# Low key parts on both halves: every score product of three attentions over 128 partitions

## The chip, the cores and the metric

The kernel runs on one core of one Trainium2 chip, in one launch. The metric is device time in microseconds (us) of that launch; lower is better. Three runs of the kernel before gave 981.36 us as their median (980.42 to 981.79). The engines are called PE (TensorE), DVE (VectorE), ACT (ScalarE), POOL (GpSimd) and SP (SyncE); PEld is PE's loading of a product's first operand, which overlaps with the products.

## The reference

Two transformer blocks over 256 tokens of 1024 numbers, in f32. The first has an attention with three branches (compressed, selected, windowed; 8 query heads, 2 key groups of 64), a recurrent branch and an MLP; the second has a neighbourhood attention (8 heads of 64), an attention over a band with a sink (8 query heads, 2 key heads), and two gated MLPs. The lines that matter here are the scores:

```python
qc = lax.dynamic_slice_in_dim(qh, t0, Q_CHUNK, axis=3)
s = jnp.einsum('bgrcd,bgcnd->bgrcn', qc, ksel) * ATTN_SCALE          # selected, first block
s = jnp.einsum('bgrcd,bgnd->bgrcn', qc, kw) * ATTN_SCALE             # windowed, first block
s = jnp.einsum('bchd,bicjhd->bhcij', q_r, k_g).astype(jnp.float32) * scale + bias   # second block, a
s = jnp.einsum('bnqhgd,bnkhd->bnhgqk', qb, kb).astype(jnp.float32) * (dh ** -0.5)   # second block, b
```

A head has 64 numbers, so each score is a sum over 64.

## The kernel before, in words

Features lie on partitions, tokens on the free axis. PE multiplies the type F32R, so each f32 operand is split in a high part (`ACT` copies it into F32R) and a low part (`DVE` subtracts the copy from the original). The weights stream in by SP's queue as pieces of 1024 columns, and `split_to` makes `whi` (ACT, L248) and `wlo` (DVE, L249) of each piece; five buffers of each hold the pieces that are split ahead. A product of features and weights is three products: high by high, low by high, high by low (L300, L294; in the MLPs L306 and L307).

**Scores.** A query tile `q(s, i)` has head s's high part on its own 64 partitions (`HALF[s]`) and its low part on the other 64, so that one product over 128 partitions with the key's high part `kh(s)`, which `put_k` writes on both halves (L585, L586, ACT), gives high by high plus low by high. The key's low part `kl` lies on head s's own half alone (L587, DVE), and the third product, high by low, runs over those 64 partitions: `q(s, i)[HALF[s]]` by `kl[HALF[s]]`. Each call of `scores2` (L767, neighbourhood attention `na_scores` and band attention `gq_scores`, four of each) makes 4 products over 128 partitions (L773) and 4 over 64 (L775); `nsa_scores` (L813) does the same for the first block, L824 and L826, with 4 and 4 (u=0, j of 4) or 2 and 2 (u=1). So there are 56 products over 128 partitions and 56 over 64, all with 256 columns. The scores of s=0 and s=1 go into the two buffers of the PSUM pool "s", which the masks (L784, DVE) read.

**Where the parts lie.** In the first block the key tile `k_1` also holds `pch` and `pcl` (the compressed attention's probabilities); `vc_parts` (tag "side") holds compressed values. In the second block `kal` lies behind the values in `va`'s two tiles, and `kb_vb` (tag "side") holds `kbh`, `kbl` and the band's values. `mix_fin` (L1247) writes the cosines and sines times the norm into a tile `cossin` of its own, which `rope_tile` reads. The pool "big" has 12 buffers of 128x2048 words.

**Order of the work.** `ORDER_1` and `ORDER_2` (L156, L159) list the steps, attention steps ("at") between projections; a scheduler that has its own model of time then sets the order on each engine.

Of the kernel before, what the change touches and what calls it, by code (L numbers as in the profile page):

```python
# [8 lines left out]
F32 = mybir.dt.float32  # L9
F32R = mybir.dt.float32r  # L10
AF = mybir.ActivationFunctionType
ALU = mybir.AluOpType
AX = mybir.AxisListType

P = 128
T = 256
# [358 lines left out]
def build(nc, tc, d, out, es, dbg=None):  # L375
# [22 lines left out]
    G = Prog(nc, tc, pools, d, dbg)  # L398
    one = pools["one"]
    V = {}  # L400
    S = {}
# [111 lines left out]
    def v2(b):  # L513
        return b.rearrange("p (k t) -> p k t", k=2)
# [67 lines left out]
    def put_k(kh, kl, t):  # L582
        for s in range(2):
            own, other = HALF[s], HALF[1 - s]
            nc.scalar.activation(out=kh(s)[own], in_=t[own], func=AF.Copy)  # L585
            nc.scalar.activation(out=kh(s)[other], in_=t[own], func=AF.Copy)  # L586
            nc.vector.tensor_tensor(out=kl[own], in0=t[own], in1=kh(s)[own].bitcast(F32), op=ALU.subtract)  # L587

    def ev_q(p, b):
        if p == 0:  # L590
# [5 lines left out]
    def ev_k(p, b):  # L596
        t = G.big("k_1", F32R, (P, 2048))
        S["kh"] = t[:, 0:1024].rearrange("p (s b t) -> p s b t", s=2, b=2)
        S["kl"] = t[:, 1024:1536].rearrange("p (b t) -> p b t", b=2)
        S["pch"], S["pcl"] = t[:, 1536:1792], t[:, 1792:2048]  # L600
        t = G.tmp("k_sb")
        nc.vector.tensor_tensor(out=v2(t), in0=v2(b), in1=two(S["rbA"]), op=ALU.mult)
        put_k(lambda s: S["kh"][:, s], S["kl"], v2(t))

    W1 = "w_in"

# [99 lines left out]
    def cmp_w2():  # L706
        hid = S["cmp_hid"]
        rep = G.tmp("cmp_rep")[:, :256].rearrange("p (h r c) -> p h r c", h=2, r=4)
        nc.vector.tensor_copy(rep, hid[:, 1, :, None, :].to_broadcast([P, 2, 4, 32]))
        b = G.ps("t", "cmpo")  # L710
        for ht in range(2):
            nc.tensor.matmul(b[:, 0:32], V["w2k"][:, ht, :], hid[:, 0, ht, :], start=ht == 0, stop=ht == 1)
        for ht in range(2):
            nc.tensor.matmul(b[:, 64:128], rep[:, ht].rearrange("p r c -> p (r c)"), V["w2v"][:, ht, :],
                             start=ht == 0, stop=ht == 1, skip_group_check=True)
        kc = b[:, 0:32].rearrange("p (s n) -> p s n", s=2)
        kl = G.small((P, 32), "kcl").rearrange("p (s n) -> p s n", s=2)
        G.split2(S["kc"][:, :, 0:16], kl, kc, 0.5)
        nc.vector.tensor_tensor(out=S["kc"][:, :, 16:32], in0=kl, in1=S["kcmask"].rearrange("p (s n) -> p s n", s=2), op=ALU.mult)
        vc = G.tmp("vc")  # L720
        nc.vector.tensor_tensor(out=vc.rearrange("p (s c) -> p s c", s=8), in0=b[:, None, 64:128].to_broadcast([P, 8, 64]),
                                in1=S["vcmask"][:, :, None].to_broadcast([P, 8, 64]), op=ALU.mult)
        t = one.tile([P, 1536], F32R, tag="side", name="vc_parts")
        S["vch"], S["vcl"] = t[:, 0:512], t[:, 512:1024]
        G.split2(S["vch"], S["vcl"], vc, 0.5)

    def gate_cols(j=None):
# [39 lines left out]
    def scores2(name, q, kh, kl):  # L767

        bs = [G.ps("s", f"S{name}{s}") for s in range(2)]
        for i in range(2):  # L770
            o = slice(i * T, i * T + T)
            for s in range(2):
                nc.tensor.matmul(bs[s][:, o], q(s, i), kh(s), start=True, stop=False, skip_group_check=True)  # L773
            for s in range(2):
                nc.tensor.matmul(bs[s][:, o], q(s, i)[HALF[s]], kl[HALF[s]], start=False, stop=True, skip_group_check=True)  # L775
        return bs

    def softmax(name, segs, post):
# [34 lines left out]
    def nsa_scores(u, j):  # L813
        nm_ = f"n{u}{j}"
        kh, kl, n = S["kh"], S["kl"], 3 if u == 0 else 1
        qs = lambda s, i: S["q"][:, s, j, i * P:(i + 1) * P]
        bs = [G.ps("s", f"S{nm_}{s}") for s in range(2)]
        if u == 0:
            parts = [(lambda s: bs[s][:, 0:T], 0, lambda k: k[:, :, 0:P]), (lambda s: bs[s][:, T:2 * T], 1, lambda k: k[:, 0, :])]
        else:  # L820
            parts = [(lambda s: bs[s][:, 0:T], 1, lambda k: k[:, 1, :])]
        for o, i, keys in parts:
            for s in range(2):
                nc.tensor.matmul(o(s), qs(s, i), keys(kh[:, s]), start=True, stop=False, skip_group_check=True)  # L824
            for s in range(2):
                nc.tensor.matmul(o(s), qs(s, i)[HALF[s]], keys(kl)[HALF[s]], start=False, stop=True, skip_group_check=True)  # L826
        first, second = S["causal"][:, 0:P], S["causal"][:, P:3 * P]
        if u == 0:
            t = pools["att"].tile([P, 2, 512], F32, tag="att", name="att" + nm_)
            segs = [(t[:, s, o:o + w], bs[s][:, o:o + w], m, False) for s in range(2)  # L830
                    for o, w, m in ((0, P, first), (P, P, first), (T, T, second))]
            g = S["gA"][:, j]
        else:
            t = pools["half"].tile([P, 2, T], F32, tag="half", name="att" + nm_)
            segs = [(t[:, s], bs[s][:, 0:T], second, False) for s in range(2)]
            g = S["gB"][:, j]

        def fin(sm):
            f = G.small((P, 2 * n), "f" + nm_)
            nc.vector.tensor_scalar(out=sm, in0=sm, scalar1=1e-20, scalar2=None, op0=ALU.max)  # L840
            nc.vector.reciprocal(f, sm)
            nc.vector.tensor_tensor(out=f, in0=f, in1=g, op=ALU.mult)
            return f

        softmax(nm_, segs, lambda nm: fin)
        S[f"at{u}{j}"] = t
# [399 lines left out]

    def mix_fin():  # L1247
        norm_fin("acc1", "A")
        cs = one.tile([P, 2, T], F32, tag="cossin", name="cossin")
        S["cossin"] = cs  # L1250
        nc.vector.tensor_tensor(out=cs[:, 0, :], in0=S["cos"], in1=S["rbA"], op=ALU.mult)
        nc.vector.tensor_tensor(out=cs[:, 1, :], in0=S["sin"], in1=S["rbA"], op=ALU.mult)

    def ev_qa(p, b):
        if p == 0:
# [5 lines left out]
    def ev_ka(p, b):  # L1261
        if p == 0:
            S["kah"] = G.big("ka", F32R, (P, 2, 4, T))
            va_ = [G.big("va" + n, F32R, (P, 2048)) for n in ("hi", "lo")]
            S["vah"], S["val"] = (v[:, 0:1536].rearrange("p (i j c) -> p i j c", i=2, j=4) for v in va_)
            S["kal"] = [v[:, 1536:2048].rearrange("p (j t) -> p j t", j=2) for v in va_]
        t = G.tmp(f"ka{p}")
        nc.vector.tensor_tensor(out=v2(t), in0=v2(b), in1=two(S["rbA"]), op=ALU.mult)
        put_k(lambda s: S["kah"][:, s, 2 * p:2 * p + 2, :], S["kal"][p], v2(t))

    def rope_tile(name, b, scale):

        t = G.tmp("rt" + name)[:, :T]
        nc.scalar.activation(out=t, in_=b, func=AF.Copy, scale=scale)
        rb = G.ps("t", "rot" + name)
        nc.tensor.matmul(rb[:, :T], S["rot"], t, start=True, stop=True)
        u = G.tmp("ru" + name)[:, :T]
        nc.vector.tensor_tensor(out=u, in0=rb[:, :T], in1=S["cossin"][:, 1, :], op=ALU.mult)
        nc.vector.tensor_tensor(out=t, in0=t, in1=S["cossin"][:, 0, :], op=ALU.mult)
        nc.vector.tensor_tensor(out=t, in0=t, in1=u, op=ALU.add)  # L1280
        return t

# [26 lines left out]

    def va():  # L1310

        sd = one.tile([P, 1536], F32R, tag="side", name="kb_vb")
        S["vbh"], S["vbl"] = (sd[:, 768 + 384 * a:1152 + 384 * a].rearrange("p (i c) -> p i c", i=2) for a in range(2))
        S["kbh"], S["kbl"] = sd[:, 0:2 * T].rearrange("p (s t) -> p s t", s=2), sd[:, 2 * T:3 * T]
        for t in (S["vah"], S["val"]):
            nc.gpsimd.memset(t[:, :, :, 64:128].bitcast(F32), 0.0)
        for t in (S["vbh"], S["vbl"]):
# [18 lines left out]
    def kb():  # L1336
        bk = G.ps("g", "kb")
        for k in range(8):
            wh, wl = G.wt(("kb", k))
            G.mmx(bk[:, :T], wh, wl, x3(k), k == 0, k == 7)  # L1340
        put_k(lambda s: S["kbh"][:, s, :], S["kbl"], rope_tile("k", bk[:, :T], 1.0))

    def full_softmax(name, bs, mask, post):
        t = pools["att"].tile([P, 2, 512], F32, tag="att", name="att" + name)
# [3 lines left out]

    def na_scores(j):
        nm_ = f"a{j}"  # L1350
        bs = scores2(nm_, lambda s, i: S["qa"][:, s, j, i * P:(i + 1) * P], lambda s: S["kah"][:, s, j, :], S["kal"][j // 2][:, j % 2, :])

        def mask(s, i):
            e = 2 if i == 0 else 0
# [10 lines left out]

    def gq_scores(j):
        nm_ = f"b{j}"
        bs = scores2(nm_, lambda s, i: S["qb"][:, s, j, i * P:(i + 1) * P], lambda s: S["kbh"][:, s, :], S["kbl"])
        sk = S["sink"].rearrange("p (s j) -> p s j", s=2)[:, :, j:j + 1].to_broadcast([P, 2, 2])

        def post(nm):
# [213 lines left out]
```

## Time and profile before

| | |
|---|---|
| median of three runs | 981.36 us |
| the profiled execution | 979.5 us |
| its span, first to last instruction | 977.7 us |
| mean granted TensorE clock | 0.996 |
| PE busy | 962.3 us (98%) |
| DVE busy | 729.8 us (75%) |
| ACT busy | 580.4 us (59%) |

The profiled execution lies 1.9 us under the median of the three runs, and 1.8 us of it lie outside the span. Busy time of PE counts overlapping products once; a product's own length is longer than the step to the next product's start, so costs on PE are read from starts. Times within the execution are us from the span's start: the first block's attention lies between 44 and 200, the second block's between 626 and 740.

### The profile page before, as it was taken

The page shows a single profiled execution, that of the slowest core. Times are in us where ns is not written, and L with a number is a line of the kernel's source. Part 1 is how long each engine was busy: PE and PEld are TensorE (multiplying, and loading weights), DVE is VectorE, ACT ScalarE, POOL GpSimd, SP SyncE. Part 2 cuts the span into 40 slices and gives each one's busy share as a digit, 9 for nine tenths or more (in the row PEclk, how much of TensorE's full clock was granted, in tenths as well). Part 3 has the DMA queues.
Part 4 walks back from the last instruction along what each step waited for, and adds up shares of the span by engine and source line. Part 5 has one row for each costly group of instructions (what it writes and reads, how often), then busy time and mean ns, then how long its engine had stood idle before and what let it go on. Part 6 is the DMA issues. An engine that isn't in the chain of part 4 may idle for free.

```text
span 977.7 us, 15978 instructions
## 1 busy us (share of the span) xinstructions
PE 962.3 (98%) x6310; PEld 874.2 (89%) x6310; DVE 729.8 (75%) x1219; ACT 580.4 (59%) x953; POOL 40.1 (4%) x71
## 2 busy tenths in 40 slices
PE   8999999999999999999999999899999999999997
PEld 7999999998888888888888889899899888888897
DVE  7898779778888655679888667678767878777553
ACT  6784897446766544556555444667664566555541
POOL 6100000000000000030000200000000000000000
PEclk9999999999999999999999999999999999999999
DMA  9584333634555545565555655353225565554541
GB/s 330 182 294 180 133 127 130 226 144 174 195 193 180 208 173 200 188 205 193 195 178 208 207 189 192 128 173 120 85 99 174 196 211 175 199 186 172 180 152 44
DMA packets 26555, 174.03 MB, mean 178 GB/s; under 512 B 3312, under 2 KB 3568, under 8 KB 7280
## 3 DMA queue, kind: packets, MB, share of 16 engines
q1 hardware_dynamic: 24912, 169.80, 49.0%
q0 software_dynamic: 1136, 2.63, 1.4%
q8 instruction: 49, 0.80, 0.3%
q10 hardware_dynamic: 432, 0.58, 0.2%
q14 instruction: 26, 0.21, 0.1%
HBM read 171.43 MB, written 1.05 MB: 176 GB/s over the span
## 4 chain that ended last, share of the span: by engine, by line
PE 97%; DVE 1%; DMA 1%; ACT 0%; issue 0%; SPq 0%; POOL 0%; POOLq 0%
PE f L306 17%; PE w L306 12%; PE f L307 8%; PE w L307 6%; PE ld L294 6%; PE ga L300 5%; PE gb L300 5%; PE fd L306 4%; PE wo L306 3%; PE gr L300 2%; PE m1b L300 2%; PE xr L300 2%; PE fd L307 2%; PE wo L307 2%; PE va L294 1%; PE ka L300 1%
## 5 line engine op out<-in xcount | busy, mean ns | idle before, releaser
L249 DVE TENSOR_TENSOR wlo<-raw,whi 128x1024 fp32r<-128x1024 f32 (+3 forms) x322 | 388.9, 1210 | 169.9 <-ACT whi L248 152.4
L248 ACT ACTIVATE whi<-raw 128x1024 fp32r<-128x1024 f32 (+3 forms) x322 | 336.0, 1048 | 301.4 <-PE w L306 64.1
L306 PE MATMUL f<-u,whi 128*128 128x512 f32 x704 | 246.7, 396 | 0.0
L307 PE MATMUL f<-u,wlo 128*128 128x256 f32 x704 | 196.9, 280 | 0.0
L306 PEld LDWEIGHTS f<-u,whi 128*128 128x128 f32 x704 | 132.2, 188 | 31.2
L307 PEld LDWEIGHTS f<-u,wlo 128*128 128x128 f32 x704 | 132.9, 189 | 0.1
L306 PE MATMUL w<-u,whi 128*128 128x512 f32 x256 | 88.8, 392 | 0.0
L306 PE MATMUL w<-hid,whi 128*128 128x512 f32 x256 | 88.8, 391 | 0.0
L307 PE MATMUL w<-hid,wlo 128*128 128x256 f32 x256 | 71.9, 281 | 0.0
L307 PE MATMUL w<-u,wlo 128*128 128x256 f32 x256 | 71.5, 281 | 0.0
L306 PE MATMUL fd<-f1h,whi 128*128 128x512 f32 x176 | 61.1, 394 | 0.0
L294 PE MATMUL ld<-whi,f2h 128*128 128x256 f32 (+1 forms) x264 | 59.1, 319 | 0.0
L306 PEld LDWEIGHTS w<-hid,whi 128*128 128x128 f32 x256 | 47.9, 187 | 10.4
L306 PEld LDWEIGHTS w<-u,whi 128*128 128x128 f32 x256 | 47.8, 187 | 10.2
L300 PE MATMUL gb<-u,whi 128*128 128x256 f32 x256 | 50.2, 288 | 0.0
L300 PE MATMUL ga<-u,whi 128*128 128x256 f32 x256 | 49.1, 287 | 0.0
L307 PE MATMUL fd<-f1h,wlo 128*128 128x256 f32 x176 | 48.9, 278 | 0.0
L307 PEld LDWEIGHTS w<-u,wlo 128*128 128x128 f32 x256 | 48.5, 190 | 0.2
L307 PEld LDWEIGHTS w<-hid,wlo 128*128 128x128 f32 x256 | 48.5, 190 | 0.0
L294 PEld LDWEIGHTS ld<-whi,f2h 128*128 128x128 f32 x264 | 44.1, 191 | 3.4
L306 PE MATMUL wo<-m,whi 128*128 128x512 f32 x128 | 44.4, 394 | 0.0
L294 PE MATMUL ld<-wlo,f2h 128*128 128x256 f32 (+1 forms) x132 | 42.1, 320 | 0.0
(534 smaller groups left out, 1919.3 us busy)
## 6 DMA issues: line engine op xcount, KB each, us to landing
raw<-in_ws_dram SPq DMA_DIRECT2D x150, 1024.0 KB, 4.9
raw<-in_ws_dram SPq DMA_DIRECT2D x3, 960.0 KB, 4.8
raw<-in_ws_dram SPq DMA_DIRECT2D x2, 992.0 KB, 4.9
nar<-in_rpb_dram POOLq DMA_DIRECT2D x16, 96.0 KB, 5.9
raw<-in_ws_dram SPq DMA_DIRECT2D x4, 256.0 KB, 6.7
raw<-in_ws_dram SPq DMA_DIRECT2D x2, 512.0 KB, 7.4
raw<-in_ws_dram SPq DMA_DIRECT2D x1, 932.0 KB, 5.3
res<-in_x_dram SPq DMA_DIRECT2D x2, 384.0 KB, 6.5
```

What stands on the lines that cost most here:

```text
L248: self.hi_ins.append(nc.scalar.activation(out=hi[:, :w], in_=src, func=AF.Copy))
L249: nc.vector.tensor_tensor(out=lo[:, :w], in0=src, in1=hi[:, :w].bitcast(F32), op=ALU.subtract)
L294: mm(out, a, b, start=start and r == 0, stop=stop and r == 2, skip_group_check=True)
L300: mm(out, a, b, start=start and r == 0, stop=stop and r == 2, skip_group_check=True)
L306: mm(bank.rearrange("p (a t) -> p a t", a=2), wh, x, start=start, stop=False, skip_group_check=True)
L307: mm(bank[:, :T], wl, x[:, 0, :], start=False, stop=stop, skip_group_check=True)
```

## The change

`put_k` writes the low part too on both halves: DVE's subtraction now comes right after the first high copy, and a new ACT copy (L588 of the changed kernel) carries it to the other half. Both kinds of scores then take all of `q(s, i)` and all of `kl(s)`, so that the second product, too, runs over 128 partitions (it adds low by low), and they go through s outside and i inside. The low parts need twice the room: `kl` of the first block takes the place of `pch` and `pcl`, which move to `vc_parts`; `kal` gets a tile of its own in the pool "big"; the tag "side" grows from 1536 to 1792 words; the cosines and sines are multiplied in place, and `cossin` goes.

```diff
@@ put_k
             nc.scalar.activation(out=kh(s)[own], in_=t[own], func=AF.Copy)
+            nc.vector.tensor_tensor(out=kl(s)[own], in0=t[own], in1=kh(s)[own].bitcast(F32), op=ALU.subtract)
             nc.scalar.activation(out=kh(s)[other], in_=t[own], func=AF.Copy)
-            nc.vector.tensor_tensor(out=kl[own], in0=t[own], in1=kh(s)[own].bitcast(F32), op=ALU.subtract)
+            nc.scalar.activation(out=kl(s)[other], in_=kl(s)[own].bitcast(F32), func=AF.Copy)
@@ ev_k
-        S["kl"] = t[:, 1024:1536].rearrange("p (b t) -> p b t", b=2)
-        S["pch"], S["pcl"] = t[:, 1536:1792], t[:, 1792:2048]
+        S["kl"] = t[:, 1024:2048].rearrange("p (s b t) -> p s b t", s=2, b=2)
@@ cmp_w2
-        t = one.tile([P, 1536], F32R, tag="side", name="vc_parts")
+        t = one.tile([P, 1792], F32R, tag="side", name="vc_parts")
         S["vch"], S["vcl"] = t[:, 0:512], t[:, 512:1024]
+        S["pch"], S["pcl"] = t[:, 1024:1280], t[:, 1280:1536]
@@ scores2
-        for i in range(2):
-            o = slice(i * T, i * T + T)
-            for s in range(2):
+        for s in range(2):
+            for i in range(2):
+                o = slice(i * T, i * T + T)
                 nc.tensor.matmul(bs[s][:, o], q(s, i), kh(s), start=True, stop=False, skip_group_check=True)
-            for s in range(2):
-                nc.tensor.matmul(bs[s][:, o], q(s, i)[HALF[s]], kl[HALF[s]], start=False, stop=True, skip_group_check=True)
+                nc.tensor.matmul(bs[s][:, o], q(s, i), kl(s), start=False, stop=True, skip_group_check=True)
@@ nsa_scores
-        for o, i, keys in parts:
-            for s in range(2):
+        for s in range(2):
+            for o, i, keys in parts:
                 nc.tensor.matmul(o(s), qs(s, i), keys(kh[:, s]), start=True, stop=False, skip_group_check=True)
-            for s in range(2):
-                nc.tensor.matmul(o(s), qs(s, i)[HALF[s]], keys(kl)[HALF[s]], start=False, stop=True, skip_group_check=True)
+                nc.tensor.matmul(o(s), qs(s, i), keys(kl[:, s]), start=False, stop=True, skip_group_check=True)
@@ mix_fin
-        cs = one.tile([P, 2, T], F32, tag="cossin", name="cossin")
...
+        for k in ("cos", "sin"):
+            nc.vector.tensor_tensor(out=S[k], in0=S[k], in1=S["rbA"], op=ALU.mult)
@@ ev_ka
-            S["kal"] = [v[:, 1536:2048].rearrange("p (j t) -> p j t", j=2) for v in va_]
+            S["kal"] = G.big("kal", F32R, (P, 2, 4, T))
@@ va
-        sd = one.tile([P, 1536], F32R, tag="side", name="kb_vb")
...
+        sd = one.tile([P, 1792], F32R, tag="side", name="kb_vb")
...
```

The orders on POOL and SP stay as they were. On PE, DVE and ACT the scheduler moves steps within the two attentions' stretches; two places matter.

PE, the scores of the neighbourhood attention's third pair of heads (`Sa`; `ka` and `valo` or `kal` are the key's high and low parts, `ga` a gate's projection beside it). Before:

```order
L300 MATMUL ga_7015<-u_0_5878,whi_6809 128x256
L773 MATMUL Sa_6988<-ka,qa 128x256
L775 MATMUL Sa_6988<-valo,qa 128x256
L773 MATMUL Sa_6988<-ka,qa 128x256
L775 MATMUL Sa_6988<-valo,qa 128x256
L773 MATMUL Sa_6989<-ka,qa 128x256
L775 MATMUL Sa_6989<-valo,qa 128x256
```

The same place in the changed kernel (its L774 and L775 are the high and the low product):

```order
L300 MATMUL ga_7021<-u_0_5880,whi_6815 128x256 x2
L774 MATMUL Sa_6994<-ka,qa 128x256
L775 MATMUL Sa_6994<-kal,qa 128x256
L774 MATMUL Sa_6994<-ka,qa 128x256
L775 MATMUL Sa_6994<-kal,qa 128x256
L300 MATMUL ga_7021<-u_0_5880,wlo_6816 128x256
L300 MATMUL ga_7021<-u_0_5880,whi_6815 128x256 x2
L300 MATMUL ga_7021<-u_0_5880,wlo_6816 128x256
L774 MATMUL Sa_6995<-ka,qa 128x256
```

High and low products alternate in both; products of the gate now stand between s=0 and s=1, and the number of score products is the same.

ACT, just after the first block's keys: weight parts (`whi`), the new copies, and the exponentials (`attn`) of the first scores. Before:

```order
L248 ACTIVATE whi_641<-raw_470 128x840
L248 ACTIVATE whi_655<-raw_535 128x840
L917 ACTIVATE xc<-xr_593,vec 128x256 x2
L248 ACTIVATE whi_675<-raw_535 128x560
L268 ACT_TABLE_LOAD
...
L268 ACTIVATE attn_1134,smn_1138<-attn_1134,nmn_1135 128x256 x2
L248 ACTIVATE whi_756<-raw_653 128x1024
L248 ACTIVATE whi_804<-raw_653 128x1024
```

The same place in the changed kernel (L588 is the new copy; buffer numbers are 2 higher):

```order
L248 ACTIVATE whi_643<-raw_472 128x840
L588 ACTIVATE k_460<-k_460 64x512 x2
L248 ACTIVATE whi_657<-raw_537 128x840
L248 ACTIVATE whi_677<-raw_537 128x560
...
L268 ACT_TABLE_LOAD
...
L248 ACTIVATE whi_758<-raw_655 128x1024
L268 ACTIVATE attn_1136,smn_1140<-attn_1136,nmn_1137 128x256
L248 ACTIVATE whi_806<-raw_655 128x1024
```

Up to `whi_804` (now `whi_806`) ACT has two copies of 64x512 more and one exponential of 128x256 less; the exponential follows later. On PE the last products of the compression's first layer (`cmph`), which use the weight part after these, now stand 16 rows of the gate's projection later.

## Rows read from the trace of the kernel before

**Rows 1.** The page: busy time of PE with its share; the chain's shares by engine.

```profile
PE 962.3 (98%) x6310; PEld 874.2 (89%) x6310; DVE 729.8 (75%) x1219; ACT 580.4 (59%) x953; POOL 40.1 (4%) x71
...
PE 97%; DVE 1%; DMA 1%; ACT 0%; issue 0%; SPq 0%; POOL 0%; POOLq 0%
```

**Rows 2.** Instructions of lines L826 and L775: count, duration (ns) min/median/max, starts.

```profile
L826 PE MATMUL Sn<-k,q x24: 379/382/382, 44.8 to 174.0; 64*128 64x256 f32 x24
...
L775 PE MATMUL Sb<-kb_vb,qb x16: 379/382/386, 683.8 to 709.0; 64*128 64x256 f32 x16
...
L775 PE MATMUL Sa<-vahi,qa x8: 380/381/383, 626.6 to 653.5; 64*128 64x256 f32 x8
...
L775 PE MATMUL Sa<-valo,qa x8: 379/380/382, 657.7 to 672.0; 64*128 64x256 f32 x8
```

**Rows 3.** Timeline of PE, third pair of `a`: start us, us, engine, line, tiles, count.

```profile
657.50 0.28 PE L773 MATMUL Sa<-ka,qa 128*128 128x256 f32 x1
657.71 0.38 PE L775 MATMUL Sa<-valo,qa 64*128 64x256 f32 x1
658.02 0.39 PE L773 MATMUL Sa<-ka,qa 128*128 128x256 f32 x1
...
659.59 0.38 PE L775 MATMUL Sa<-valo,qa 64*128 64x256 f32 x1
...
660.12 0.28 PE L300 MATMUL ga<-u,wlo 128*128 128x256 f32 x1
660.24 0.40 PE L300 MATMUL ga<-u,whi 128*128 128x256 f32 x2
```

**Rows 4.** Timeline of PE, scores of the first block at 163.

```profile
162.82 0.40 PE L824 MATMUL Sn<-k,q 128*128 128x256 f32 x2
163.15 0.39 PE L826 MATMUL Sn<-k,q 64*128 64x256 f32 x2
163.46 0.51 PE L824 MATMUL Sn<-k,q 128*128 128x256 f32 x2
163.90 0.38 PE L826 MATMUL Sn<-k,q 64*128 64x256 f32 x2
...
164.55 0.28 PE L300 MATMUL gb<-u,wlo 128*128 128x256 f32 x1
```

**Rows 5.** Timeline of PE: first and last of the rows with two 64-partition products.

```profile
45.38 0.38 PE L826 MATMUL Sn<-k,q 64*128 64x256 f32 x2
...
690.55 0.39 PE L775 MATMUL Sb<-kb_vb,qb 64*128 64x256 f32 x2
```

**Rows 6.** Timeline of PE, 50 to 62; in brackets idle time and its releaser.

```profile
50.92 0.40 PE L294 MATMUL vg<-wlo,u 128*128 128x280 f32 x1 [0.32 <-DVE wlo L249]
...
58.93 0.50 PE L300 MATMUL ga<-u,whi 128*128 128x256 f32 x2
...
61.37 0.34 PE L673 MATMUL cmph<-whi,cmpB 128*64 128x256 f32 x1 [1.09 <-ACT whi L248]
```

**Rows 7.** Timeline of ACT: a key copy, an exponential, two weight pieces.

```profile
42.23 0.63 ACT L586 ACTIVATE k<-k_sb 64x512 fp32r<-64x512 f32 x1
...
56.33 0.49 ACT L268 ACTIVATE attn<-attn,nmn 128x256 f32<-128x256 f32 x1
...
56.87 2.01 ACT L248 ACTIVATE whi<-raw 128x1024 fp32r<-128x1024 f32 x2
```

**Rows 8.** Busy time by stretch: length; PE, PEld, DVE, ACT, POOL; clock, DMA.

```profile
50.00:75.00 25.00, 23.59 (x188) 22.73 (x188) 24.97 (x48) 20.70 (x40) 1.50 (x4) 1.00 0.85 307
150.00:175.00 25.00, 25.00 (x196) 23.64 (x195) 24.62 (x52) 21.32 (x40) 0.00 (x0) 1.00 0.44 158
```

**Rows 9.** ACT's longest wait in 62 to 175: total us, times, longest.

```profile
ACT whi L248 <- PE xr L300: 5.2, 3, 3.0
```

**Rows 10.** Timeline of PE behind its longest wait in the second block.

```profile
619.15 0.77 PE L300 MATMUL ka<-u,whi 128*128 128x256 f32 x2 [3.31 <-DVE qa L1258]
```

**Rows 11.** Writers of tile `tga`, 640 to 740: count, duration, first and last start.

```profile
L1411 DVE SCALAR_TENSOR_TENSOR tga<-ga,rb_A x3: 682/692/693, 666.6 to 694.9; 128x512 f32<-128x512 f32 x3
```

More of the change, by code (lines that the diff above doesn't have):

```diff
@@ L598, in ev_k @@
         S["kh"] = t[:, 0:1024].rearrange("p (s b t) -> p s b t", s=2, b=2)
-        S["kl"] = t[:, 1024:1536].rearrange("p (b t) -> p b t", b=2)
-        S["pch"], S["pcl"] = t[:, 1536:1792], t[:, 1792:2048]
+        S["kl"] = t[:, 1024:2048].rearrange("p (s b t) -> p s b t", s=2, b=2)
         t = G.tmp("k_sb")
         nc.vector.tensor_tensor(out=v2(t), in0=v2(b), in1=two(S["rbA"]), op=ALU.mult)
-        put_k(lambda s: S["kh"][:, s], S["kl"], v2(t))
+        put_k(lambda s: S["kh"][:, s], lambda s: S["kl"][:, s], v2(t))
     W1 = "w_in"
@@ L1248, in mix_fin @@
         norm_fin("acc1", "A")
-        cs = one.tile([P, 2, T], F32, tag="cossin", name="cossin")
-        S["cossin"] = cs
-        nc.vector.tensor_tensor(out=cs[:, 0, :], in0=S["cos"], in1=S["rbA"], op=ALU.mult)
-        nc.vector.tensor_tensor(out=cs[:, 1, :], in0=S["sin"], in1=S["rbA"], op=ALU.mult)
+        for k in ("cos", "sin"):
+            nc.vector.tensor_tensor(out=S[k], in0=S[k], in1=S["rbA"], op=ALU.mult)
     def ev_qa(p, b):
@@ L1265, in ev_ka @@
             S["vah"], S["val"] = (v[:, 0:1536].rearrange("p (i j c) -> p i j c", i=2, j=4) for v in va_)
-            S["kal"] = [v[:, 1536:2048].rearrange("p (j t) -> p j t", j=2) for v in va_]
+            S["kal"] = G.big("kal", F32R, (P, 2, 4, T))
         t = G.tmp(f"ka{p}")
         nc.vector.tensor_tensor(out=v2(t), in0=v2(b), in1=two(S["rbA"]), op=ALU.mult)
-        put_k(lambda s: S["kah"][:, s, 2 * p:2 * p + 2, :], S["kal"][p], v2(t))
+        put_k(lambda s: S["kah"][:, s, 2 * p:2 * p + 2, :], lambda s: S["kal"][:, s, 2 * p:2 * p + 2, :], v2(t))
     def rope_tile(name, b, scale):
@@ L1277, in rope_tile @@
         u = G.tmp("ru" + name)[:, :T]
-        nc.vector.tensor_tensor(out=u, in0=rb[:, :T], in1=S["cossin"][:, 1, :], op=ALU.mult)
-        nc.vector.tensor_tensor(out=t, in0=t, in1=S["cossin"][:, 0, :], op=ALU.mult)
+        nc.vector.tensor_tensor(out=u, in0=rb[:, :T], in1=S["sin"], op=ALU.mult)
+        nc.vector.tensor_tensor(out=t, in0=t, in1=S["cos"], op=ALU.mult)
         nc.vector.tensor_tensor(out=t, in0=t, in1=u, op=ALU.add)
@@ L1310, in va @@
     def va():
-        sd = one.tile([P, 1536], F32R, tag="side", name="kb_vb")
-        S["vbh"], S["vbl"] = (sd[:, 768 + 384 * a:1152 + 384 * a].rearrange("p (i c) -> p i c", i=2) for a in range(2))
-        S["kbh"], S["kbl"] = sd[:, 0:2 * T].rearrange("p (s t) -> p s t", s=2), sd[:, 2 * T:3 * T]
+        sd = one.tile([P, 1792], F32R, tag="side", name="kb_vb")
+        S["vbh"], S["vbl"] = (sd[:, 1024 + 384 * a:1408 + 384 * a].rearrange("p (i c) -> p i c", i=2) for a in range(2))
+        S["kbh"], S["kbl"] = (sd[:, 512 * a:512 * a + 512].rearrange("p (s t) -> p s t", s=2) for a in range(2))
         for t in (S["vah"], S["val"]):
@@ L1340, in kb @@
             G.mmx(bk[:, :T], wh, wl, x3(k), k == 0, k == 7)
-        put_k(lambda s: S["kbh"][:, s, :], S["kbl"], rope_tile("k", bk[:, :T], 1.0))
+        put_k(lambda s: S["kbh"][:, s, :], lambda s: S["kbl"][:, s, :], rope_tile("k", bk[:, :T], 1.0))
     def full_softmax(name, bs, mask, post):
@@ L1350, in na_scores @@
         nm_ = f"a{j}"
-        bs = scores2(nm_, lambda s, i: S["qa"][:, s, j, i * P:(i + 1) * P], lambda s: S["kah"][:, s, j, :], S["kal"][j // 2][:, j % 2, :])
+        bs = scores2(nm_, lambda s, i: S["qa"][:, s, j, i * P:(i + 1) * P], lambda s: S["kah"][:, s, j, :], lambda s: S["kal"][:, s, j, :])
         def mask(s, i):
@@ L1367, in gq_scores @@
         nm_ = f"b{j}"
-        bs = scores2(nm_, lambda s, i: S["qb"][:, s, j, i * P:(i + 1) * P], lambda s: S["kbh"][:, s, :], S["kbl"])
+        bs = scores2(nm_, lambda s, i: S["qb"][:, s, j, i * P:(i + 1) * P], lambda s: S["kbh"][:, s, :], lambda s: S["kbl"][:, s, :])
         sk = S["sink"].rearrange("p (s j) -> p s j", s=2)[:, :, j:j + 1].to_broadcast([P, 2, 2])
```

## The prediction

> **What bounds the kernel now.** I read the page first. PE is busy for 98% of the span and the chain of work that ended last runs through PE for 97% of it [rows 1]: whatever shortens the row of products shortens the kernel, as long as the other engines keep ahead. Next, the instructions of the two low product lines: 56 products over 64 partitions, each 0.38 us long [rows 2]. That length says little, since products overlap; the timeline of PE gives the steps from start to start. Two neighbouring products over 128 partitions with 256 columns start 0.12 us apart (660.12 and 660.24 in [rows 3]). Around a low product this is different: the step into it is 0.21 us, the step out of it 0.31 us [rows 3]. Where two low products stand side by side, one on each half, a row with both is as long as one alone, 0.38 or 0.39 us [rows 4, 5], so they run at the same time; but the way in and out is paid there too. Last come the waits and busy times by stretch, which tell where PE has a margin. The list of PE's waits is empty between 62 and 175 and between 625 and 710, while ACT waits for PE there to hand back weight buffers [rows 9]: PE sets the pace. Between 44 and 62 it does not: PE waits 0.32 us for a low weight part and 1.09 us for a high one [rows 6], with DVE busy 24.97 of 25 us in the stretch from 50 [rows 8].
>
> **The sum, part by part.** *A low product that stands alone.* From 657.50 to 660.12 there are 8 score products, four of them lone low ones, and one gate product: 2.62 us [rows 3]. Nine steps of 0.12 make 1.08. The other 1.54 us are four visits to half height, 0.385 us each.
>
> *Two that stand together.* From 162.82 to 164.55 there are 8 score products with two such couples, and two gate products: 1.73 us [rows 4]. Ten steps make 1.20, so a couple costs 0.53 / 2 = 0.265 us more than two full products would.
>
> The Trainium skill's page "TensorEngine Tiling (Array Packing)", Key Properties, says that changing the tiling mode drains TensorE; by that rule the cost sits at the change of height, and the steps of 0.21 and 0.31 us agree.
>
> *How many.* Twelve rows of the timeline hold a couple, the first at 45.38 and the last at 690.55 [rows 5]; the other 32 of the 56 stand alone. They fall in three stretches: 4 alone and 1 couple up to 51 (1.54 + 0.27 = 1.8 us), 12 alone and 3 couples from 96 to 174 (4.62 + 0.80 = 5.4 us), 16 alone and 8 couples from 626 to 709 (6.16 + 2.12 = 8.3 us). The sum is 15.5 us.
>
> In the changed kernel all 56 are full products behind a full product with the same first operand. The trace has none of exactly this kind. The bounds are 0.12 us, the step of any full product into the same bank, and 0.31 us, the step at a low one. I take 0.12: first and second operand then have the shape of the gate's products, whose step that is.
>
> *The last two stretches.* I let 5.4 and 8.3 us count whole: 13.7 us. The cover is that weight parts, probabilities and masks must come 6 or 7% sooner there. ACT's waits for PE of up to 3.0 us [rows 9] are room of that kind; the tightest stretch is 150 to 175, with DVE busy 24.62 of 25 us [rows 8]. New waits of some tenths are likely and are in the range, not in the sum.
>
> *The first stretch.* Here PE gains 1.8 us and gives nearly all back. ACT makes the weight part that PE takes at 58.93 as the second of two that end at 56.87 + 2.01 = 58.88 [rows 6, 7]; PE uses it as soon as it is there. The change puts two new copies of 64x512 ahead of it, 0.63 us each by the copy it resembles, and takes one exponential of 0.49 us out from before it [rows 7]: 0.77 us later, at 59.65. PE arrives earlier and waits. In exchange the product that waited 1.09 us at 61.37 now stands 16 rows later, by which time its part is there. Net: 1.09 - 0.77 = 0.3 us gained. Its ends are a loss of 1.3 us (both copies delay PE in full) and a gain of 1.8 + 0.32 + 1.09 = 3.2 us (the visits and both waits go).
>
> *The rest.* Six more ACT copies lie in the second block: four of 64x512 at 0.63 us, two of 64x256 at no more than that, under 4 us on an engine that is busy 59% of the span; PE's weight parts lie far ahead there (no PE wait in 625 to 710), so nothing. If that cover were gone, at most these 4 us. Of the subtractions none is added; they stand one copy earlier. The cosines and sines take the same two multiplications. The low keys' own tile is a thirteenth claim on the 12 buffers when the gate's tile `tga` comes. That is first written at 666.6 [rows 11]; the first bias tile, whose buffer it then takes, is read for the last time by the masks of the second pair of heads, before the third pair's scores at 657.50 can use their banks [rows 3]: 9 us of margin, cost nothing. POOL and SP keep their order.
>
> Together 5.4 + 8.3 + 0.3 = 14.0 us. The profiled execution took 979.5 us, so it becomes 965.5. The median shown, 981.36, lies 1.9 us above that execution; against it I predict **967.4 us**.
>
> **The rivals.** *A, the first block does not follow.* DVE is full from 150 to 175 [rows 8]; if masks, probabilities and low weight parts cannot come sooner, PE meets its new slack as waits, and the 5.4 us between 96 and 174 are lost. For it: the 24.62 of 25 us. Against it: no wait of PE in that stretch now, and ACT waiting for PE's buffers [rows 9]. Time: 981.4 - 8.3 - 0.3 = 972.8 us.
>
> *B, the steps stay.* The 0.31 us could come not from the height but from something that the change keeps: a second accumulation into the bank just written, or the alternation of high and low keys. Then all 56 are lone ones: 24 more of 0.385, against 12 couples of 0.265 less, 9.24 - 3.18 = 6.1 us slower: 987.4 us. It decides from a step of about 0.2 us after a low product; below that the couples weigh less. Against it: projections accumulate into one bank too, at 0.12 us [rows 3], and in [rows 4] the two high products side by side, at 162.82, share one 0.40 us row like any two full ones. The same page of the Trainium skill, Theoretical Speedup, promises up to twice the rate for sums of up to 64 numbers; by that the change gives something up. The rows show it for the 12 couples alone: each spares one step of 0.12 us, 1.4 us in all, against 15.5 for getting there and back.
>
> *C, the first stretch gets worse.* The copies delay PE in full, 1.3 us, and PE's waits there bunch. Behind the 3.31 us wait at 619 two products took 0.77 us [rows 10] where two take 0.40 [rows 3]; something like that again would cost about 1 us more. Time: 967.4 + 0.3 + 1.3 + 1 = 970 us.
>
> **How the numbers follow.** The forecast has 0.77: its terms are counted on steps that the timeline shows, and its open part is whether PE stays the bound. A has 0.13, C 0.05, B 0.03, and 0.02 is for no change within what a measurement of this kernel can tell, 0.2% or 2 us. The range goes down to the whole 15.5 us and both waits of the first stretch, 981.4 - 16.9 = 964.5; up to 972.5, which takes in C and all of A but its worst edge. Faster by over 0.2%: 0.77 + 0.13 + 0.05 = 0.95; same 0.02; slower 0.03.
>
> **What would show it.** Right: the low product lines read 128x256 with about 0.28 us each, starting 0.12 us behind their neighbours; the eight products of the third pair of heads take about 1 us instead of 2.4; PE busy about 948 us, its share still 98%; PE's waits between 50 and 62 grow by about 1.5 us in all, and none above 1 us appears between 62 and 175 or between 625 and 710. Wrong: steps of 0.2 us or more at the low products (B), PE waits of several us for DVE between 96 and 200 (A), long products behind a wait near 60 (C), or a wait of the gate's tile for a buffer.

## The result and the profile after

The changed kernel takes 966.12 us (median of 4 runs, 965.93 to 968.79). Beside it, the kernel before takes 981.18 us (median of 4, 980.42 to 981.79); the ratio is 0.9853, with a 95% interval of 0.9835 to 0.9872. Predicted were 967.4 us. The profiled execution took 966.17 us with a span of 964.4; the one before took 979.5 and 977.7. The medians thus differ by 15.1 us and the two profiled executions by 13.3, because the one before is a quick execution of its kernel and the one after lies at its kernel's median.

The page's busy time of PE and the chain by engine, after:

```profile
PE 948.3 (98%) x6310; PEld 870.1 (90%) x6310; DVE 728.4 (76%) x1219; ACT 585.0 (61%) x961; POOL 42.0 (4%) x71
...
PE 93%; ACT 4%; DVE 1%; issue 1%; DMA 0%; POOL 0%; POOLq 0%; ACTq 0%
```

PE has the same 6310 products as in [rows 1] and is busy 14.0 us less. Its share stays at 98%, so the end moved with it. The chain now runs through ACT for 4%: in the first block it goes back from a short wait of PE at 149.19 through ACT's work to 125, and before that through ACT around 40 to 48. The low products of the neighbourhood attention and of the first block, with their shapes and durations (ns min/median/max):

```profile
L775 PE MATMUL Sa<-kal,qa x16: 281/283/283, 621.5 to 663.8; 128*128 128x256 f32 x16
...
L825 PE MATMUL Sn<-k,q x24: 274/283/388, 48.4 to 169.4; 128*128 128x256 f32 x24
```

They have the full height, and take 0.28 us where [rows 2] has 0.38. The timeline of PE shows the steps, here for the third pair of heads (start us, us, engine, line, tiles):

```profile
650.42 0.28 PE L774 MATMUL Sa<-ka,qa 128*128 128x256 f32 x1
650.54 0.28 PE L775 MATMUL Sa<-kal,qa 128*128 128x256 f32 x1
650.66 0.28 PE L774 MATMUL Sa<-ka,qa 128*128 128x256 f32 x1
650.78 0.28 PE L775 MATMUL Sa<-kal,qa 128*128 128x256 f32 x1
650.90 0.28 PE L300 MATMUL ga<-u,wlo 128*128 128x256 f32 x1
...
651.38 0.28 PE L774 MATMUL Sa<-ka,qa 128*128 128x256 f32 x1
```

From 650.42 on every step is 0.12 us, high to low and low to high alike, and so is the step into the gate's product. The same eight products at half height are [rows 3].

Where the gain lies is read from two marks that both kernels have: the first product of `wo` behind the first block's attention, and the first product of `f` behind the second block's (line, starts of first and last product). Before:

```profile
L306 PE MATMUL wo<-m,whi x64: 390/392/405, 212.7 to 234.6; 128*128 128x512 f32 x64
...
L306 PE MATMUL f<-u,whi x352: 392/398/478, 782.5 to 906.9; 128*128 128x512 f32 x176
```

After:

```profile
L306 PE MATMUL wo<-m,whi x64: 389/391/403, 207.6 to 229.5; 128*128 128x512 f32 x64
...
L300 PE MATMUL ka<-u,wlo x32: 278/283/420, 604.9 to 621.3; 128*128 128x256 f32 x32
...
L306 PE MATMUL f<-u,whi x352: 392/398/477, 769.2 to 893.6; 128*128 128x512 f32 x176
```

The first stretch and the first block gave 212.7 - 207.6 = 5.1 us, the second block (782.5 - 769.2) - 5.1 = 8.2. The rest of the program takes as long as before. The last product of `ka`, at 621.3, is a third mark; from it to the first of `f` the second block takes 147.9 us.

PE's longest waits after (us in total, times, longest):

```profile
PE ka L300 <- DVE qa L1255: 3.3, 1, 3.3
...
PE ga L300 <- ACT whi L248: 1.1, 1, 1.1
...
PE cmph L673 <- ACT whi L248: 0.4, 1, 0.4
PE o L869 <- ACT pt100h L329: 0.2, 1, 0.2
```

The first stands in the kernel before, too [rows 10]. The next two are the first stretch; the timelines of PE and ACT there, after:

```profile
58.33 0.33 PE L673 MATMUL cmph<-whi,cmpB 128*64 128x256 f32 x1 [0.41 <-ACT whi L248]
59.77 0.50 PE L300 MATMUL ga<-u,whi 128*128 128x256 f32 x2 [1.10 <-ACT whi L248]
```

```profile
47.72 1.28 ACT L588 ACTIVATE k<-k 64x512 fp32r<-64x512 f32 x2
...
57.24 1.04 ACT L248 ACTIVATE whi<-raw 128x1024 fp32r<-128x1024 f32 x1
58.19 0.49 ACT L268 ACTIVATE attn<-attn,nmn 128x256 f32<-128x256 f32 x1
58.68 1.04 ACT L248 ACTIVATE whi<-raw 128x1024 fp32r<-128x1024 f32 x1
```

The two copies and the exponential that now stands between the pieces bring the part that PE took at 58.93 [rows 6] to 58.68 + 1.04 = 59.72, and PE takes it at 59.77. The last wait in the list is new: at 149.19 PE needs probabilities that ACT makes behind an activation of the recurrent branch.

```profile
147.72 1.04 ACT L268 ACTIVATE rg<-rg 128x1024 f32<-128x1024 f32 x1
148.67 0.47 ACT L329 ACTIVATE pt100h<-ptn 128x384 fp32r<-128x384 f32 x1
149.04 0.48 ACT L329 ACTIVATE pt101h<-ptn 128x384 fp32r<-128x384 f32 x1
```

### The profile page after: what moved, and what is told of

Its sections match the earlier page's. It is cut to its first block, busy times and chain, and to the rows that moved or that the text cites. A ratio compares the mean times of both kernels' runs of the same rounds, so it can differ in the third digit from the quotient of the medians.

```text
span 964.4 us, 15990 instructions
## 1 busy us (share of the span) xinstructions
PE 948.3 (98%) x6310; PEld 870.1 (90%) x6310; DVE 728.4 (76%) x1219; ACT 585.0 (61%) x961; POOL 42.0 (4%) x71
## 4 chain that ended last, share of the span: by engine, by line
PE 93%; ACT 4%; DVE 1%; issue 1%; DMA 0%; POOL 0%; POOLq 0%; ACTq 0%
PE f L306 17%; PE w L306 12%; PE f L307 9%; PE w L307 6%; PE ld L294 6%; PE ga L300 5%; PE fd L306 4%; PE gb L300 4%; PE wo L306 3%; PE m1b L300 2%; PE fd L307 2%; PE xr L300 2%; PE gr L300 2%; PE wo L307 2%; PE va L294 1%; PE ka L300 1%
## 5 line engine op out<-in xcount | busy, mean ns | idle before, releaser
L307 PEld LDWEIGHTS w<-hid,wlo 128*128 128x128 f32 x256 | 48.4, 189 | 0.0
L300 PE MATMUL gb<-u,whi 128*128 128x256 f32 x256 | 48.2, 284 | 0.0
```

The lines of the kernel that those rows point to most:

```text
L300: mm(out, a, b, start=start and r == 0, stop=stop and r == 2, skip_group_check=True)
L307: mm(bank[:, :T], wl, x[:, 0, :], start=False, stop=stop, skip_group_check=True)
```

## The experiments

Two theories were open. By the first the gain is the changes of height alone (a visit is the way from full to half height and back), 0.385 us for a low product between full ones and 0.265 for a couple, and each stretch gives its own. By the rivals it is in part the order (s outside), the number of products of half height, or a wait that goes; and what the first stretch frees is eaten by the new copies on ACT. The diffs are against the changed kernel unless another is named.

**The two blocks apart.** `e1_second` has the change in the second block alone, `e2_first` in the first alone; the other block's scores stand as before.

```diff
@@ e1_second, nsa_scores (put_k, kl, pch and pcl of the first block as before)
-        for s in range(2):
-            for o, i, keys in parts:
+        for o, i, keys in parts:
+            for s in range(2):
...
-                nc.tensor.matmul(o(s), qs(s, i), keys(kl[:, s]), start=False, stop=True, skip_group_check=True)
+            for s in range(2):
+                nc.tensor.matmul(o(s), qs(s, i)[HALF[s]], keys(kl)[HALF[s]], start=False, stop=True, skip_group_check=True)
```

> Second block's scores alone over 128 partitions; the first block's keys and scores as in the kernel before. Theory (the price sits at each change of height on PE, and PE is the bound in both attentions): the second block's 8 couples and 16 lone visits go, 8.2 us, so about 973.0 us, with the first block's products where they stood before. Rival (the gain comes mostly from elsewhere, such as the freed tile of cosines or the order on DVE and ACT): not the share by visits, but under 6 or over 11 us.

> First block's scores alone over 128 partitions; the second block as in the kernel before. Theory: 12 lone visits and 3 couples after 62 us go, 5.4 us, and the first stretch gives nearly nothing, since ACT's new copies and the weight parts decide there: 5.1 to 5.7 us, about 976 us. Rival (the first stretch's 1.8 us count as well): 7.2 us, about 974 us.

Measured: 972.0 us for the second block alone (971.06 to 972.83; ratio 0.9907, 0.9892 to 0.9922) and 974.78 for the first alone (974.61 to 977.01; 0.9942, 0.9925 to 0.996), with the kernel before at 980.84 beside them. That is 8.8 and 6.1 us, together 14.9, against 14.7 for both (980.84 - 966.12). The parts add up; neither needs the other. The 6.1 lies above the 5.1 to 5.7 expected and under the rival's 7.2. By the marks of the profiles `e1_second` is 148.0 us long from the last product of `ka` to the first of `f`, the kernel before 782.5 - 626.2 = 156.3: 8.3 us. `e2_first` gains 212.7 - 207.9 = 4.8 us up to `wo`. Its transposes behind the first stretch (the compression's) start at 74.7 where the kernel before has 74.6: the first stretch gave nothing there, and the excess of the medians is within the spread of the runs.

**The order alone.** `e4_order` is the kernel before with s outside and i inside, at half height: 52 low products stand alone and 2 couples are left.

```diff
@@ against the kernel before: scores2, and likewise nsa_scores
-        for i in range(2):
-            o = slice(i * T, i * T + T)
-            for s in range(2):
+        for s in range(2):
+            for i in range(2):
+                o = slice(i * T, i * T + T)
...
-            for s in range(2):
```

> The kernel before with only the order of the score products changed, s outside and i inside, each low product behind its high one; low products stay on 64 partitions. The built order then has 52 lone low products and 2 couples where before it had 32 and 12. Theory (visits to half height are paid, 0.385 us alone, 0.265 us as a couple): 20 x 0.385 - 10 x 0.265 = 5.1 us slower than the kernel before, about 986 us. Rival (the new order, with the same first operand twice in a row, is what makes the change faster): faster than before by several us.

Measured: 985.62 us (985.0 to 986.51; 1.0047, 1.0032 to 1.0062), 4.8 slower than before. The order gains nothing by itself; it costs what breaking ten couples into twenty lone products costs, 20 x 0.385 - 10 x 0.265 = 5.05 us. In its second block 30 lone products and 1 couple stand where there were 16 and 8, which makes 11.8 - 8.3 = 3.5 us; between the same marks it takes 788.0 - 628.2 = 159.8 us, 3.5 more than the 156.3 of the kernel before.

**One low product in four back at half height**, in the second block: eight lone visits.

```diff
@@ scores2
-                nc.tensor.matmul(bs[s][:, o], q(s, i), kl(s), start=False, stop=True, skip_group_check=True)
+                h = HALF[s] if s and i else slice(0, P)
+                nc.tensor.matmul(bs[s][:, o], q(s, i)[h], kl(s)[h], start=False, stop=True, skip_group_check=True)
```

> The changed kernel with one low product in four of the second block (s=1, i=1) put back to 64 partitions: 8 lone visits, same order of the loops, same copies, same tiles. Theory: 8 x 0.385 = 3.1 us slower than the changed kernel, about 969.2 us, and the steps at these 8 products are 0.21 us in and 0.31 us out while all others stay 0.12 us. Rival (height does not matter, the order does): no change, 966.1 us.

Measured: 969.86 us (969.27 to 971.69; 0.9888, 0.9874 to 0.9903), 3.7 above the changed kernel. One of the visits in the timeline of PE, and the two marks:

```profile
650.00 0.28 PE L774 MATMUL Sa<-ka,qa 128*128 128x256 f32 x1
650.21 0.38 PE L776 MATMUL Sa<-kal,qa 64*128 64x256 f32 x1
650.52 0.39 PE L300 MATMUL qb<-u,wlo 128*128 128x256 f32 x1
650.74 0.40 PE L300 MATMUL qb<-u,whi 128*128 128x256 f32 x2
```

```profile
L300 PE MATMUL ka<-u,wlo x32: 280/283/415, 606.3 to 623.7; 128*128 128x256 f32 x32
...
L306 PE MATMUL f<-u,whi x352: 392/398/477, 774.7 to 899.1; 128*128 128x512 f32 x176
```

The steps are 0.21 us in and 0.31 out, as expected, and the step behind is 0.22: together 0.38 more than three steps of 0.12. The same product at full height, in the same order on PE, with the same copies and tiles, costs none of it. Between the last product of `ka` and the first of `f` lie 774.7 - 623.7 = 151.0 us, where the changed kernel has 147.9. That is 3.1 us for eight visits, 0.38 each. The 0.6 that the medians differ by beyond that is less than the spread of its runs, for which the last section has a reason.

**Half height, grouped.** `e6_group` is the kernel before, with all high products of a call first and its low ones behind them in one group, held in that order on PE. In it the second high product into a bank starts a sum of its own there while the first one's is still open, and the scores come out without part of their terms; the work on PE is the same. `e6b_group` lets only the first product into each bank start, in both blocks, and leaves nothing out.

```diff
@@ e6b_group against the kernel before: scores2 (the same in nsa_scores; e6_group has start=True)
+        for i in range(2):
+            o = slice(i * T, i * T + T)
+            for s in range(2):
+                ins.append(nc.tensor.matmul(bs[s][:, o], q(s, i), kh(s), start=i == 0, stop=False, skip_group_check=True))
+        for i in range(2):
+            o = slice(i * T, i * T + T)
+            for s in range(2):
+                ins.append(nc.tensor.matmul(bs[s][:, o], q(s, i)[HALF[s]], kl[HALF[s]], start=False, stop=True, skip_group_check=True))
+        for a, b in zip(ins, ins[1:]):
+            G.behind(b, a)
```

> The kernel before, low products on 64 partitions, but each unit's high products first and all its low ones behind them, in couples (an order without waits is set between the products; other work may still stand between). The built order has 10 groups of four, 1 of three, 6 of two and 1 lone product. Theory (the price is the change of height, and couples run at the same time): a group of four costs 0.385 - 2 x 0.12 = 0.145 us, two or three 0.265, one 0.385: 3.7 us over full height, less what the first stretch hides, and ACT has no new copies: 968.5 to 969.5 us. Rival (every couple costs 0.31 us however they stand): 10 x 0.19 = 1.9 us more, about 971 us. Second rival (couples pay as the tiling page promises and entry is cheap when grouped): at or under 966 us.

> The second block at half height with the high products first and the four low ones grouped behind them, as before, but only the first product into each score bank starts a sum. Instructions, shapes and order on PE are those of the grouped run, so its time is to be the same: 969 to 970 us, 3 to 4 above the changed kernel (eight visits of one lone one and a couple less their two steps). Rival: the second start into the bank cost something of its own; then it is up to 1 us faster.

Measured: 969.56 us (969.12 to 970.35; 0.9885, 0.987 to 0.9899) and 969.4 (967.43 to 970.4; 0.988, 0.9867 to 0.9893), the same time, at the upper end of what was expected. The timeline of PE in `e6_group`, third pair, and its two marks:

```profile
653.40 0.52 PE L774 MATMUL Sa<-ka,qa 128*128 128x256 f32 x3
653.85 0.50 PE L778 MATMUL Sa<-valo,qa 64*128 64x256 f32 x4
...
654.51 0.28 PE L300 MATMUL ga<-u,wlo 128*128 128x256 f32 x1
```

```profile
L300 PE MATMUL ka<-u,wlo x32: 281/283/415, 606.5 to 622.9; 128*128 128x256 f32 x32
...
L306 PE MATMUL f<-u,whi x352: 392/398/477, 772.5 to 896.9; 128*128 128x512 f32 x176
```

Three high and four low products and one gate product behind them take 653.40 to 654.51, 1.11 us; eight full ones would take 0.96. The four low ones, two on each half, take two steps and not four, which pays for most of one way in and out: 0.15 us too much for a whole call, against about 1.5 for its four lone visits. In the second block `e6_group` is 772.5 - 622.9 = 149.6 us long, 1.7 more than the changed kernel; its six groups of four, one of three, one couple and one lone product make 1.8 by the prices. So the price is that of the change of height, not of the half height. Full height still beats the grouping, by some 3.3 us in all. The Trainium skill's page "TensorEngine Tiling (Array Packing)", Key Properties, puts a drain at a change of tiling mode, and not at a change of the tile alone; a visit of four products on both tiles for 0.15 us agrees.

**The first stretch, without the copies.** `e3_zeros` leaves out the ACT copies of the low key parts; POOL sets the other halves to zero instead, so low by low is left out of the scores.

```diff
@@ put_k, ev_k, ev_ka, and likewise for kbl
+    def zero_other(kl):
+        for s in range(2):
+            nc.gpsimd.memset(kl[HALF[1 - s], s].bitcast(F32), 0.0)
-            nc.scalar.activation(out=kl(s)[other], in_=kl(s)[own].bitcast(F32), func=AF.Copy)
+        zero_other(S["kl"])
```

> The changed kernel without ACT's eight new copies: the low key parts' other halves are set to zero by POOL ahead of time, so the low products run over 128 partitions but leave low by low out, as in the kernel before. Theory (in the first stretch ACT's two copies of 0.63 us, less one exponential moved behind, hold PE up by 0.77 us at the weight part taken near 59; all other copies are hidden): 0.5 to 1.3 us faster than the changed kernel, about 965.2 us, with PE taking that weight part near 59.0 and not at 59.8. Rival (the copies are hidden everywhere and PE's wait near 59 has another cause): no change, 966.1 us.

Measured: 966.61 us (964.45 to 967.29; 0.9856, 0.984 to 0.9872): a miss, the same as with the copies. PE's waits in its first stretch, and the weight part that was expected sooner:

```profile
49.87 0.35 PE L828 MATMUL Sn<-k,q 128*128 128x256 f32 x1 [0.83 <-DVE cmpB L330]
50.85 0.39 PE L294 MATMUL vg<-wlo,u 128*128 128x280 f32 x1 [0.51 <-DVE wlo L249]
...
58.93 0.50 PE L300 MATMUL ga<-u,whi 128*128 128x256 f32 x2
...
61.37 0.33 PE L677 MATMUL cmph<-whi,cmpB 128*64 128x256 f32 x1 [1.10 <-ACT whi L248]
```

One part of what was expected came true: PE takes that part at 58.93, 0.84 us sooner than the changed kernel and exactly where the kernel before did. It gains nothing by it, for the scheduler also gave ACT back its order of before and PE most of it, with the `cmph` product in front of the gate's again, and that one waits until 61.37, to the hundredth as in the kernel before [rows 6]. The time that PE no longer spends on visits comes back as waits for DVE around 50. So without the copies other waits eat the 1.8 us; but the run changes the order along with the copies, and what the copies cost in the changed kernel's own order stays open.

Busy time from 50 to 62 (length; PE, PEld, DVE, ACT, POOL; clock, DMA), in the changed kernel and in `e3_zeros`:

```profile
50.00:62.00 12.00, 10.36 (x80) 9.66 (x79) 11.17 (x28) 11.97 (x26) 0.00 (x0) 1.00 0.77 264
```

```profile
50.00:62.00 12.00, 10.39 (x79) 9.73 (x80) 11.95 (x24) 11.97 (x29) 0.00 (x0) 1.00 0.75 266
```

ACT is full in both, and as full, 11.97 of 12 us, in the kernel before; PE waits for its work in all three.

**The first stretch, exponentials moved.** If not the copies, then perhaps the exponentials that ACT makes ahead of and between the two weight pieces at 57.24 and 58.68. `e8_ahead` holds the first eight of them behind both pieces; in `e8_ahead2` the index is 22 for the first six, so that only the first piece goes ahead of these, and 23 for the other two (its expectation says three).

```diff
@@ table
         ins = self.nc.scalar.activation(**kw)
+        if "accum_out" in kw and self.n_exp < 8:
+            self.behind(ins, self.hi_ins[23])
+            self.n_exp += 1
```

> The changed kernel with one order edited on ACT: the first eight exponentials of the first block's attention stand behind two weight pieces that stood among them; PE keeps its order. Theory: the exponentials ahead of these pieces on ACT, not the new copies, eat the 1.8 us that full height frees up to 51 us. Then PE's waits of 0.4 and 1.1 us for ACT near 58 and 60 go, the compression's transposes start 0.7 to 1.5 us sooner than the changed kernel's 74.47, and the time is 964.6 to 965.4 us against its 966.1. Rival: the next weight pieces, whose loads wait for buffers, are late next; the two waits come back between 60 and 75 as one of about a microsecond, the transposes start at 74.5 and the time stays at 966.1 or is up to 1 us longer.

> As the run before, in a milder form: the first of the two weight pieces ahead of all eight exponentials, the second ahead of the last three. Theory: the 0.4 us wait goes, the 1.1 us wait goes or shrinks to 0.3, and 965 us. Rival as there: the transposes stay at 74.5 and the time at 966.1.

Measured: 974.08 us (971.76 to 976.65; 0.9929, 0.9914 to 0.9944) and 972.04 (969.55 to 974.02; 0.9906, 0.9892 to 0.992), 8 and 6 us slower than the changed kernel, more than either theory allowed. ACT and PE in `e8_ahead`, first stretch:

```profile
54.38 2.01 ACT L249 ACTIVATE whi<-raw 128x1024 fp32r<-128x1024 f32 x2 [1.17 <-DMA raw<-in_ws_dram]
```

```profile
59.44 0.39 PE L304 MATMUL ga<-u,wlo 128*128 128x256 f32 x1 [0.51 <-DVE wlo L250]
63.28 0.33 PE L677 MATMUL cmph<-whi,cmpB 128*64 128x256 f32 x1 [0.45 <-ACT whi L249]
68.76 0.51 PE L304 MATMUL xr<-u,whi 128*128 128x256 f32 x2 [0.56 <-ACT gates L637]
```

The pieces were made earlier, but ACT first waited 1.17 us for their load, and PE's waits came back as three of about half a microsecond, 1.5 us as before. The transposes start at 75.0, not sooner than 74.47. In `e8_ahead2` PE has one wait for a weight part instead, of 2.35 us at 60.48, the granted clock falls behind it (0.72 from 60 to 66), and the transposes start at 76.5. Here the rival held in its outcome: in neither order did the stretch get shorter.

The larger loss lies elsewhere. The scheduler laid the attention steps after 75 us out anew, and so these runs are not an edit of ACT's order alone. The profiled `e8_ahead` is 8.3 us behind that of the changed kernel: 3.0 at the first product of `wo`, and 4.2 more up to 415, of which the last section tells. PE and ACT near 160 in it:

```profile
160.56 0.73 PE L873 MATMUL o<-pt101h,v 128*128 128x512 f32 x2 [2.57 <-ACT pt101h L333]
```

```profile
149.63 1.28 ACT L269 ACT_TABLE_LOAD   x1
...
155.33 1.28 ACT L269 ACT_TABLE_LOAD   x1
...
160.03 0.47 ACT L333 ACTIVATE pt101h<-ptn 128x384 fp32r<-128x384 f32 x1
```

The recurrent branch's activations (`rt`, `rg`) and table loads hold ACT from 149.63 to 156.6. In the changed kernel they are done at 148.8 and `pt101h` follows at 149.04; here it comes at 160.03, behind them and behind further work. PE waits 2.57 us, 3.26 in `e8_ahead2`. In the changed kernel the wait of 0.19 us at 149.19 is a small one of the same kind.

## Why the prediction was right, and where it was off

*Steps.* 0.12 us for a full product behind one with the same first operand: so it is everywhere in the timeline above, the lower of the two bounds. The prices of a visit are shown by three runs that use them on other numbers of visits: 0.38 a lone one (`e5_one_half`), 4.8 us for the order that breaks the couples (5.05 by the prices), 1.7 us for the grouping in the second block (1.8 by the prices). The two steps that the text names, 0.21 and 0.31, make up only 0.28 of a lone visit's 0.385; the rest is the step after them, 0.22, which the sum over the whole pair had in it.

*Second block.* 8.3 us forecast, 8.2 measured.

*First stretch and first block.* 0.3 + 5.4 = 5.7 us forecast, 5.1 measured; this is the term that was off, and the reason why the execution took 966.17 us and not 965.5. The compression's transposes behind the first stretch start at 74.47, before at 74.61, but 0.09 of these 0.14 us are there already at the first score product (44.34, before 44.43). The stretch itself gave 0.05 of its 0.3, though the part forecast for 59.65 came only 0.12 late, at 59.77. At 149.19 PE waits 0.19 us for probabilities, and the two products behind the wait take 0.73 us where two such take 0.63. These make some 0.5 of the 0.7 that is missing from the 44th microsecond on; the rest was not found. Rival A's loss of 5.4 us did not come. The 0.2 us are a wait for ACT, and A had looked at DVE.

*The median* was forecast as 1.9 us above the profiled execution, as in the kernel before; it lies 0.05 under it. So 967.4 is 1.3 us too slow although the gain within the execution was put 0.7 us too high: two errors of opposite sign, and that the sum came so near is partly luck. The granted clock bears on it. Seven runs of the kernel before, made beside the experiments, had a mean clock of 0.996 and took 979.6 to 980.14 us, and its runs at 0.994 or 0.995 took 980.65 to 982.72. The changed kernel took 966.1 and 966.2 at 0.996. At equal clock the gain is thus 13.4 to 14.1 us, where 14.0 were forecast.

*The reason given for the first stretch* describes this kernel's order, but is not shown as the cause. The text said that PE gives its 1.8 us back because two copies stand ahead of a weight part. `e3_zeros` has no copies and gives it back all the same, in another order; `e8_ahead` makes the weight parts ahead of the exponentials and gives it back too. The text named DVE as the full engine, 24.97 of 25 us [rows 8]; but from 50 to 62 ACT is the one that is full in the kernel before, the changed one and `e3_zeros` alike, 11.97 of 12 us, while DVE's 11.97 fell to 11.17 with the change. That ACT's work bounds the stretch is read from this and not shown by a run; what would loosen it was not tried.

*Rival B* fell with the steps. *Rival C*: long products behind a wait near 60 do not occur in the changed kernel's profile, but they do in that of `e5_one_half`, below; the 1.3 us for the copies never came.

*What else was named.* PE busy 948 us: 948.3. No wait above 1 us between 62 and 175 or 625 and 710: none. PE's waits between 50 and 62 should have grown by 1.5 us. This sign did not come: they went from 0.32 + 1.09 to 0.41 + 1.10, 0.1 us more. The rest of the growth stands ahead of 50, where the low products waited 0.6 us, in two pieces, for the new copies (L588), up to 48.4 and up to 49.2. The gate's tile waits for no buffer.

## What to carry to other kernels

Price a product by the step to its neighbours' starts, not by its length, and price a half-height product by the way in and out: alone between full products it cost four times a full step here, so filling the idle half with a term that adds little was cheaper than sparing it. Where half height is wanted, put its products side by side in one group. And where PE is freed in a stretch that lives on another engine's supply, count little for it, whatever wait happens to be written there; look for the next one in the queue before you name the cause.

## What the runs showed of the chip beyond that

*The granted clock fell in some kernels and not in others where PE's work was alike.* Busy time by stretch (length; PE, PEld, DVE, ACT, POOL; clock, DMA). Around PE's 3.3 us wait for `qa`, in the changed kernel, in `e3_zeros` and in `e5_one_half`:

```profile
600.00:625.00 25.00, 21.69 (x166) 21.52 (x165) 18.44 (x29) 14.93 (x21) 1.66 (x3) 0.93 0.36 123
```

```profile
600.00:625.00 25.00, 21.69 (x176) 21.52 (x174) 19.04 (x33) 14.44 (x20) 3.55 (x5) 1.00 0.37 123
```

```profile
600.00:625.00 25.00, 21.69 (x160) 21.52 (x159) 17.57 (x27) 13.73 (x19) 1.66 (x3) 0.86 0.42 143
```

PE idles the same 3.3 us in all three. Behind it the clock fell to its lower level, 1.2 GHz, for a part of the stretch in the first, for twice that in the third, and not at all in the second. In `e5_one_half` it also fell at 60, behind the wait of 1.10 us that this kernel shares with the changed one, whose clock stayed at 1.00 there (first `e5_one_half`, then the changed kernel):

```profile
60.00:66.00 6.00, 5.89 (x37) 5.64 (x37) 6.00 (x10) 5.49 (x10) 0.00 (x0) 0.72 0.68 224
```

```profile
60.00:66.00 6.00, 5.88 (x49) 5.62 (x49) 6.00 (x11) 5.54 (x10) 0.00 (x0) 1.00 0.64 231
```

With the fall 37 products start in 6 us, without it 49: 12 steps of 0.12, 1.4 us. A fall more or less is therefore worth 1 to 2 us, which is of the size of the spread between runs of one kernel. The longer fall at 600 and the one at 60 can account for the profile of `e5_one_half` (971.69 us) being its slowest run, 2.4 us behind its quickest; no trace shows the quicker ones, so this is argued.

*Long products have two lengths at one granted clock.* The second MLP half of the first block, in the changed kernel and in `e8_ahead`, both with the clock at 1.00 from 230 to 420:

```profile
L306 PE MATMUL w<-hid,whi x256: 391/391/391, 319.4 to 407.8; 128*128 128x512 f32 x128
```

```profile
L310 PE MATMUL w<-hid,whi x256: 395/398/403, 324.9 to 415.0; 128*128 128x512 f32 x128
```

The same products over the same tiles take 88.4 us from first to last start in the one and 90.1 in the other. The `f` products after the second block show the longer form before and after alike (398 in the rows of the first section). What sets it stays open. From the first product of `wo` to the last of these, `e8_ahead` takes 415.0 - 210.6 = 204.4 us and the changed kernel 407.8 - 207.6 = 200.2; PE's waits name 0.2 us of the 4.2, and the longer form, which all three groups of products in this stretch have (`wo` and both halves of the MLP), would make up the rest. It is half of what `e8_ahead` lost.
